# Order of the seven block products in the mLSTM query and key pairs

## The chip, the cores and the metric

The kernel runs on one core of a Trainium2 chip. The metric is device time of one execution, in microseconds (us). An engine works through its own list of instructions in the order in which the program put them; lists of different engines are tied together by semaphores. PE is the matrix engine, ACT the scalar engine, DVE the vector engine, SP the engine that issues the DMAs.

## The reference

The reference is one layer of a hybrid encoder block on 1024 tokens of width 1024, in float32. What matters here is its mLSTM branch: queries and keys are a projection of the normalised input, go through a causal convolution over four tokens and a SiLU, and then enter a chunkwise recurrence, four heads of width 128. Gates from the same projection scale the branches before they are merged.

```python
z = h @ w_in[i]
qa, ka, va, qk_m, vm, om, if_pre, ga, gb = jnp.split(z, split_pts, axis=-1)
...
qk_m = jax.nn.silu(causal_dwconv(qk_m, conv_m_w[i]))
qm, km = jnp.split(qk_m, 2, axis=-1)
...
hm = mlstm_chunkwise(qm.reshape(B, S, ML_HEADS, ML_DIM),
                     km.reshape(B, S, ML_HEADS, ML_DIM) * (ML_DIM ** -0.5),
                     vm.reshape(B, S, ML_HEADS, ML_DIM), i_pre, logf)
hm = head_layernorm(hm, ml_norm_g[i]) * jax.nn.sigmoid(om).reshape(B, S, ML_HEADS, ML_DIM)
```

## The kernel before, in words

Activations lie feature by token: 128 features on the partitions, 1024 tokens along the free axis, in two halves of 512. Two output tiles of 128 features are computed together, as a **pair**: for head h the query tile is row 0 of the pair, the key tile row 1. With the two halves of the tokens a pair has four outputs, (row, half). The pair is a 2x2 block product done with seven products (Strassen and Winograd's scheme) in place of eight. Each of the seven (`B11`, `T1`, `T2`, `B21`, `T3`, `B22`, `T4`) is a sum of 12 matmuls of 128x128 by 128x512: four blocks of the inner dimension, each three times (L379 weight high part by input high part, L380 weight high by input low, L381 weight low by input high), since every float32 operand is split into a high part (`wh`, by ACT, L121) and a remainder (`wl`, by DVE, L122).

`products` (L365) runs the seven on three PSUM banks. `B11`, then `T2`, `T3` and `T4` add into bank `b2`; `T1` and then `B22` into `b3`; `B21` into `b4`. The running sum in `b2` is read between them: after `B11` ACT copies it to the tile `s1`, after `T2` to `u2`, after `T3` DVE adds it to `s5` (the copy of `T1`), after `T4` it is an output. The outputs become complete with `B21` (row 0, half 0), `T3` (row 1, half 1), `B22` (row 0, half 1) and `T4` (row 1, half 0).

`left_operands` (L322) makes the weight side of each product in the order in which the products stand: it loads the four 128x512 weight blocks A11, A21, A22 and A12 of a pair into tiles `wr` (five buffers), forms the sums S1 to S4 on DVE (L292), and splits each operand into `wh` and `wl`, for which there are three buffers each. The eighth product of a stream of pairs thus reuses the buffer of the fifth.

`c_blocks` (L851) takes the four outputs. For a query and key pair (`make_qk`, L864) each output starts a convolution on DVE in `conv_silu` (L871, L874, and L877 for the tokens at the seam of the halves), a sigmoid on ACT (L880) and a product (L292 for queries, L884 for keys), into the tiles `cv`, one for the query and one for the key. The second half of a row needs the last three tokens of its first half. The key's second half lies in `s5` and waits until `T4` gives the first half, which ACT copies to the tile `c`. The tiles `s1`, `u2`, `s5` and `c` have one buffer each; the pair that comes next writes its own `s1` into the same place.

Each query and key pair is followed by a **gate pair** (two gate tiles, also by `c_blocks`), and that by the mLSTM head, whose scores `pS` (L941) multiply key by query. The first four scores need only the first halves of both. A scheduler sets the order of the instructions of each engine when the kernel is built; it moves instructions of independent work between each other, so that the scores stand inside the gate pair. There are four query and key pairs, at about 380, 451, 519 and 587 us.

Of the kernel before, what the change touches and what calls it, by code (L numbers as in the profile page):

```python
# [45 lines left out]
LO_M = "DDDDDDD"  # L46
# [8 lines left out]
T_Q, T_K, T_VA, T_QM, T_KM, T_VM, T_OM, T_GA, T_GB = 0, 4, 8, 12, 16, 20, 24, 28, 36  # L55
# [14 lines left out]
def block_kernel(ctx: ExitStack, tc: tile.TileContext, a: dict, out: bass.AP):  # L70
# [27 lines left out]
    def v(name, i=0, n=1):  # L98
        lo = _VEC_COLS[name][0] + i
        return vec[:, lo:lo + n]  # L100

    def acc(name):
        return pools["acc"].tile([P, HALF], F32, tag="acc", name=name)
# [9 lines left out]
    def half_slice(half):  # L113
        return slice(half * HALF, (half + 1) * HALF)
# [170 lines left out]
    BLOCKS_BY_USE = ("B11", "T1", "T2", "B21", "T3", "B22", "T4")  # L285
# [5 lines left out]
    def tt(eng, out, in0, in1, op):  # L291
        eng.tensor_tensor(out=out, in0=in0, in1=in1, op=op)  # L292

    def copy(out, ps):
        ACT.activation(out=out, in_=ps, func=AF.Copy)
# [8 lines left out]
    def new_blocks(n=KD // 2):  # L304
        return {m: [None] * n for m in BLOCKS}
# [16 lines left out]
    def left_operands(jobs):  # L322

        for src1, src2, n, engs, order in jobs:
            if src2 is None:
                for blk in order:
                    yield load_pre((src1, blk), n)
                continue

            def load(src):  # L330
                t = wr.tile([P, 4, P], F32, tag="wr", name="wr")[:, :n]
                SP.dma_start(out=t, in_=src)
                return t

            def comb(name, in0, in1, op=ALU.subtract):
                t = ws(n, name)
                tt(DVE, t, in0, in1, op)
                return t

            A11, A21, A22, A12 = load(src1[:, :n]), load(src2[:, :n]), load(src2[:, n:]), load(src1[:, n:])  # L340
            for blk in order:
                if blk == "T1":
                    S1 = comb("S1", A21, A22, ALU.add)
                    S2 = comb("S2", S1, A11)
                elif blk == "T3":
                    S3 = comb("S3", A11, A21)
                elif blk == "B22":
                    S4 = comb("S4", A12, S2)
                src = {"B11": lambda: A11, "T1": lambda: S1, "T2": lambda: S2, "B21": lambda: A12,
                       "T3": lambda: S3, "B22": lambda: S4, "T4": lambda: A22}[blk]()  # L350
                yield w_split(src, POOL if engs[BLOCKS_BY_USE.index(blk)] == "P" else DVE)
# [3 lines left out]
    def next_w():  # L355
        while len(w_queue) < 3:
            w_queue.append(next(left[0], None))
        return w_queue.pop(0)

    def start_products(jobs):  # L360

        left[:] = [left_operands(jobs)]
        w_queue[:] = [next(left[0]) for _ in range(2)]

    def products(blocks, order=BLOCKS_BY_USE):  # L365

        bank = {b: acc(b) for b in ("b2", "b3", "b4")}
        for blk in order:
            b = {"T1": "b3", "B22": "b3", "B21": "b4"}.get(blk, "b2")
            more = blk not in ("B11", "T1", "B21")
            w, rhs, n = next_w(), blocks[blk], len(blocks[blk])
            kw = dict(skip_group_check=True) if more else {}
            for k in range(n):
                (wh, wl), (xh, xl) = w[k], rhs[k]
                PE.matmul(bank[b], wh, xh, start=(k == 0 and not more), stop=False, **kw)  # L379
                PE.matmul(bank[b], wh, xl, start=False, stop=False, **kw)  # L380
                PE.matmul(bank[b], wl, xh, start=False, stop=(k == n - 1), **kw)  # L381
            yield blk, bank[b]
# [184 lines left out]
    with tc.tile_pool(name="att", bufs=1) as at:  # L567
# [210 lines left out]
        blocks = [(h, qb) for h in range(H) for qb in range(NTB)]  # L778
# [29 lines left out]
    zb = new_blocks()  # L808
# [18 lines left out]


    GATE_PAIRS = [(T_GA + 4, T_GA + 5), (T_GA + 6, T_GA + 7)] + [(T_GB + j, T_GB + j + 1) for j in range(0, KD, 2)]
    pair_jobs = [(T_QM, T_KM), GATE_PAIRS[0]]  # L830
    for h in range(H):
        pair_jobs.append((T_OM + h, T_GA + h))
        if h + 1 < H:
            pair_jobs.append((T_QM + h + 1, T_KM + h + 1))
        pair_jobs += GATE_PAIRS[h + 1:h + 2] if h + 1 < H else GATE_PAIRS[h + 1:]
    start_products([(a["w_in"][t1], a["w_in"][t2], 4, LO_M, BLOCKS_BY_USE) for t1, t2 in pair_jobs])

    hm_hl = [], []
    merged = new_blocks()
# [8 lines left out]
    def s_tile(tag, bufs=1):  # L848
        return mw.tile([P, HALF], F32, tag=tag, name=tag, bufs=bufs)

    def c_blocks(blocks, ready):  # L851

        s1, u2, s5 = s_tile("s1"), s_tile("u2"), s_tile("s5")
        for blk, ps in products(blocks):
            if blk in ("B11", "T1", "T2"):
                copy({"B11": s1, "T1": s5, "T2": u2}[blk], ps)
            elif blk == "T4":
                ready(1, 0, ps)
            else:
                t, row, half = {"B21": (s1, 0, 0), "T3": (s5, 1, 1), "B22": (u2, 0, 1)}[blk]  # L860
                tt(DVE, t, ps, t, ALU.add)
                ready(row, half, t)

    def make_qk(h):  # L864
        cvs = [mw.tile([P, S], F32, tag="cv", name="cv", bufs=3) for _ in range(2)]
        z = {}

        def conv_silu(row, half, prev):
            o, zt = cvs[row][:, half_slice(half)], z[row, half]
            i = h + 4 * row  # L870
            DVE.tensor_scalar(out=o, in0=zt, scalar1=v("cm", i * 4 + 3), scalar2=None, op0=ALU.mult)  # L871
            for j in (2, 1, 0):
                d, w = 3 - j, v("cm", i * 4 + j)
                DVE.scalar_tensor_tensor(out=o[:, d:], in0=zt[:, :HALF - d], scalar=w, in1=o[:, d:],  # L874
                                         op0=ALU.mult, op1=ALU.add)
                if half:
                    DVE.scalar_tensor_tensor(out=o[:, :d], in0=prev[:, HALF - d:], scalar=w, in1=o[:, :d],  # L877
                                             op0=ALU.mult, op1=ALU.add)
            sg = s_tile("sg", 2)
            ACT.activation(out=sg, in_=o, func=AF.Sigmoid)  # L880
            if row == 0:
                tt(DVE, o, o, sg, ALU.mult)
            else:
                DVE.scalar_tensor_tensor(out=o, in0=o, scalar=P ** -0.5, in1=sg, op0=ALU.mult, op1=ALU.mult)  # L884

        def ready(row, half, t):
            z[row, half] = t
            if row == 0:
                conv_silu(row, half, z[0, 0])
            elif half == 0:  # L890
                c21 = z[1, 0] = s_tile("c")
                copy(c21, t)
                conv_silu(1, 0, None)
                conv_silu(1, 1, c21)

        c_blocks(zb, ready)
        return cvs

    def gate_out(t, half, val):
# [7 lines left out]
    def gate_pair(t1, t2, om=None):  # L907

        def ready(row, half, t):
            if row == 0 and om is not None:  # L910
                ACT.activation(out=om[:, half_slice(half)], in_=t, func=AF.Sigmoid)
                return
            val = s_tile("c") if (row, half) == (1, 0) else t
            ACT.activation(out=val, in_=t, func=AF.Sigmoid)
            gate_out((t1, t2)[row], half, val)

        c_blocks(zb, ready)
# [71 lines left out]
    def mlstm_out(h, num):  # L989
# [11 lines left out]
        return om  # L1001

    qks = [make_qk(0)]
    gate_pair(*GATE_PAIRS[0])
    for h in range(H):
        num = mlstm_head(h)
        om = mlstm_out(h, num)
        if h + 1 < H:
            qks.append(make_qk(h + 1))
            gate_pair(*GATE_PAIRS[h + 1])  # L1010
    for h in range(H - 1):
# [6 lines left out]
    for c, parts in zip((H0, H1), hm_hl):  # L1018
        hi = mw.tile([P, HALF], F32R, tag="sg", name="hmh", bufs=2)
        split(hi, lo[:, c], om[:, c], lo_eng=DVE)  # L1020
        parts.append((hi, lo[:, c]))
    for pair in GATE_PAIRS[H:]:
        gate_pair(*pair)
# [409 lines left out]
```

## Time and profile before

| | us |
|---|---|
| three timed runs, median | 1595.6 |
| lowest and highest | 1594.05, 1598.84 |
| the profiled execution | 1594.36 |
| its span, first to last instruction | 1592.6 |
| PE busy in the span | 1544.1 |
| DVE busy | 1262.9 |
| ACT busy | 750.5 |

The profiled execution lies 1.2 us under the median and 1.8 us over its own span. Matmuls are pipelined: in a busy stretch they start closer together than one of them lasts, so time is read from starts.

### The profile page before, as it was taken

To read this page: it belongs to the slowest core of one execution; us is meant where nothing else is said; L and a number is where in the kernel's file an instruction comes from. 1 tells how busy PE (TensorE), PEld (TensorE's weight loads), DVE (VectorE), ACT (ScalarE), POOL (GpSimd) and SP (SyncE) were. 2 spreads that over 40 slices of the span, in tenths; PEclk is the share of its full clock that TensorE was granted. 3 is DMA by queue.
4 is the path that set the end of the run, shared out by engine and by line. 5 is a ranking of instruction groups with operands and counts; after the bars stand their busy time and mean duration, and the time that the engine had idled before them with its cause. 6 is when DMAs were issued, how large, how long until landed. Compare 5 with 4: busy or idle time off the path is not lost.

```text
span 1592.6 us, 21503 instructions
## 1 busy us (share of the span) xinstructions
PE 1544.1 (97%) x7413; PEld 1272.1 (80%) x7413; DVE 1262.9 (79%) x2193; ACT 750.5 (47%) x1448; POOL 26.0 (2%) x22
## 2 busy tenths in 40 slices
PE   8999999989999999999999999999999899999997
PEld 6777777867778788787877888888888778788997
DVE  6797885585888878759796888888888997878745
ACT  3465553444475564534365444444444635344522
POOL 0000000000000000000000000000000000000000
PEclk8999999989999999999999999999999999999999
DMA  5655641084424232465426333333333755332422
GB/s 188 193 172 172 199 143 41 21 281 150 132 74 140 95 116 86 139 225 181 149 88 223 106 106 106 105 101 99 100 100 106 244 160 185 106 131 60 136 88 90
DMA packets 117180, 212.58 MB, mean 133 GB/s; under 512 B 13840, under 2 KB 27728, under 8 KB 117072
## 3 DMA queue, kind: packets, MB, share of 16 engines
q1 hardware_dynamic: 116496, 210.70, 41.0%
q8 instruction: 58, 0.95, 0.3%
q10 hardware_dynamic: 576, 0.52, 0.1%
q14 instruction: 50, 0.41, 0.1%
HBM read 147.96 MB, written 59.02 MB: 130 GB/s over the span
## 4 chain that ended last, share of the span: by engine, by line
PE 71%; DVE 14%; DMA 6%; issue 4%; ACT 3%; SPq 1%; POOL 1%; DVEq 0%; POOLq 0%; ACTq 0%
PE b L381 18%; PE b L379 18%; PE b L380 17%; PE ps_pg L1333 2%; PE ps_pg L1335 2%; PE ps_pg L1334 2%; DVE wl L122 2%; DVE cv L874 1%; DVE mg L292 1%; PE pav L755 1%; PE ps_ya L150 1%; PE ps_ya L151 1%; PE ps_ya L152 1%; DVE nmax L728 1%; PE ps_s L706 1%
## 5 line engine op out<-in xcount | busy, mean ns | idle before, releaser
L379 PE MATMUL b<-T,wh 128*128 128x512 f32 x816 | 319.2, 391 | 6.6 <-ACT wh L121 2.8
L381 PE MATMUL b<-T,wl 128*128 128x512 f32 x816 | 318.9, 391 | 1.8 <-DVE wl L122 1.8
L380 PE MATMUL b<-T,wh 128*128 128x512 f32 x816 | 318.3, 390 | 0.0
L379 PE MATMUL b<-B,wh 128*128 128x512 f32 x612 | 239.9, 392 | 1.5 <-ACT wh L121 1.4
L381 PE MATMUL b<-B,wl 128*128 128x512 f32 x612 | 239.4, 391 | 1.2 <-DVE wl L122 0.7
L380 PE MATMUL b<-B,wh 128*128 128x512 f32 x612 | 238.5, 390 | 0.0
L121 ACT ACTIVATE wh<-S 128x512 fp32r<-128x512 f32 (+1 forms) x204 | 126.7, 621 | 233.9 <-PE b L380 209.8
L379 PEld LDWEIGHTS b<-T,wh 128*128 128x128 f32 x816 | 153.5, 188 | 41.4 <-ACT wh L121 4.6
L381 PEld LDWEIGHTS b<-T,wl 128*128 128x128 f32 x816 | 153.5, 188 | 35.6 <-DVE wl L122 3.6
L380 PEld LDWEIGHTS b<-T,wh 128*128 128x128 f32 x816 | 153.4, 188 | 32.1
L121 ACT ACTIVATE wh<-wr 128x512 fp32r<-128x512 f32 (+1 forms) x153 | 94.8, 621 | 163.5 <-PE b L380 105.9
L122 DVE TENSOR_TENSOR wl<-S,wh 128x512 fp32r<-128x512 f32 (+1 forms) x204 | 137.8, 676 | 39.3 <-ACT wh L121 38.1
L381 PEld LDWEIGHTS b<-B,wl 128*128 128x128 f32 x612 | 114.9, 188 | 26.5 <-DVE wl L122 1.9
L379 PEld LDWEIGHTS b<-B,wh 128*128 128x128 f32 x612 | 114.9, 188 | 26.4 <-ACT wh L121 2.2
L380 PEld LDWEIGHTS b<-B,wh 128*128 128x128 f32 x612 | 114.9, 188 | 23.7
L122 DVE TENSOR_TENSOR wl<-wr,wh 128x512 fp32r<-128x512 f32 (+1 forms) x153 | 103.3, 675 | 7.7 <-ACT wh L121 7.7
L292 DVE TENSOR_TENSOR x<-b,x 128x512 f32<-128x512 f32 x112 | 77.1, 689 | 34.5 <-PE b L381 34.1
L292 DVE TENSOR_TENSOR S<-wr 128x512 f32<-128x512 f32 (+1 forms) x102 | 69.1, 677 | 5.2 <-DMA wr<-w_o 3.3
L1169 DVE SCALAR_TENSOR_TENSOR ac<-ar,vec,ac 128x511 f32<-128x511 f32 (+1 forms) x88 | 65.8, 747 | 0.7
L709 ACT ACTIVATE e<-ps_s,nmax 128x128 f32<-128x128 f32 (+7 forms) x64 | 47.1, 738 | 35.3 <-DVE nmax L728 21.0
L1333 PE MATMUL ps_pg<-x,wpg 128*128 128x384 f32 (+1 forms) x192 | 61.3, 319 | 0.0
L1335 PE MATMUL ps_pg<-x,wpg 128*128 128x384 f32 (+1 forms) x192 | 61.0, 318 | 0.0
(309 smaller groups left out, 2810.4 us busy)
## 6 DMA issues: line engine op xcount, KB each, us to landing
wr<-w_up SPq DMA_DIRECT2D x84, 256.0 KB, 2.9
wr<-w_in SPq DMA_DIRECT2D x56, 256.0 KB, 3.0
pre<-pr SPq DMA_DIRECT2D x46, 256.0 KB, 2.3
wf<-w_in SPq DMA_DIRECT2D x32, 256.0 KB, 3.2
wr<-w_down SPq DMA_DIRECT2D x32, 256.0 KB, 2.8
wh<-pre SPq DMA_DIRECT2D x23, 256.0 KB, 4.2
wl<-pre SPq DMA_DIRECT2D x23, 256.0 KB, 4.5
xt<-xT SPq DMA_DIRECT2D x8, 512.0 KB, 6.6
```

The lines of the kernel that those rows point to most:

```text
L121: ACT.activation(out=hi, in_=src, func=AF.Copy)
L122: (lo_eng or DVE).tensor_tensor(out=lo, in0=src, in1=hi.bitcast(F32), op=ALU.subtract)
L150: PE.matmul(ps, wh, xh, start=(first and k == 0), stop=False)
L292: eng.tensor_tensor(out=out, in0=in0, in1=in1, op=op)
L379: PE.matmul(bank[b], wh, xh, start=(k == 0 and not more), stop=False, **kw)
L380: PE.matmul(bank[b], wh, xl, start=False, stop=False, **kw)
L381: PE.matmul(bank[b], wl, xh, start=False, stop=(k == n - 1), **kw)
L709: ACT.activation(out=e, in_=s_, func=AF.Exp, bias=nm[:, m:m + 1], scale=1.0, accum_out=rs[:, m:m + 1])
L1169: DVE.scalar_tensor_tensor(out=o[:, d:], in0=ar[:, j + d:j + HALF], scalar=v("cf", t * 3 + j), in1=o[:, d:], op0=ALU.mult, op1=ALU.add)
L1333: PE.matmul(pg, wh, xh[:, c], start=(i == 0), stop=False)
L1334: PE.matmul(pg, wh, xl[:, c], start=False, stop=False)
L1335: PE.matmul(pg, wl, xh[:, c], start=False, stop=(i == KD - 1))
```

## The change

The query and key pairs take their seven products in another order: `T3` and `T4`, which complete the key's two outputs, come before `B21` and `B22`, which complete the query's. All other pairs keep their order. The weight side is made in the new order too, since `left_operands` follows it.

```diff
@@ -827,13 +827,16 @@
+    QK_ORDER = ("B11", "T1", "T2", "T3", "T4", "B21", "B22")
     pair_jobs = [(T_QM, T_KM), GATE_PAIRS[0]]
...
-    start_products([(a["w_in"][t1], a["w_in"][t2], 4, LO_M, BLOCKS_BY_USE) for t1, t2 in pair_jobs])
+    start_products([(a["w_in"][t1], a["w_in"][t2], 4, LO_M, BLOCKS_BY_USE if t1 >= T_OM else QK_ORDER)
+                    for t1, t2 in pair_jobs])
...
-    def c_blocks(blocks, ready):
+    def c_blocks(blocks, ready, order=BLOCKS_BY_USE):
 
         s1, u2, s5 = s_tile("s1"), s_tile("u2"), s_tile("s5")
-        for blk, ps in products(blocks):
+        for blk, ps in products(blocks, order):
...
-        c_blocks(zb, ready)
+        c_blocks(zb, ready, QK_ORDER)
         return cvs
```

The number of instructions of each engine stays the same; their order changes in four places of the program, once for each query and key pair. In the rows below a name is a tile and its number, and `b2_4500<-T3_3648,wh_4522` reads: into bank `b2` of this pair, from the input block `T3` and the weight `wh`. The rows are from the second pair (head 1). Line numbers of the change are three higher than those of before from L831 on.

**First place: PE at the end of `T2`.** Before, the 12 matmuls of `B21` follow as a block:

```order
L381 MATMUL b2_4500<-T2_3592,wl_4504 128x512
L379 MATMUL b4_4502<-B21_3632,wh_4520 128x512
L380 MATMUL b4_4502<-B21_3632,wh_4520 128x512
L381 MATMUL b4_4502<-B21_3632,wl_4521 128x512
L379 MATMUL b4_4502<-B21_3636,wh_4520 128x512
```

Now two matmuls of `B21` (those that need only `wh`) stand first, then `T3`:

```order
L381 MATMUL b2_4500<-T2_3592,wl_4504 128x512
L379 MATMUL b4_4502<-B21_3632,wh_4556 128x512
L380 MATMUL b4_4502<-B21_3632,wh_4556 128x512
L379 MATMUL b2_4500<-T3_3648,wh_4522 128x512
L380 MATMUL b2_4500<-T3_3648,wh_4522 128x512
```

Behind these, PE now has the rest of `T3`'s 12, four of `B21`, all 12 of `T4`, the last six of `B21` and the 12 of `B22`. `B21`'s weight, the fourth operand of the pair before, is now the sixth.

**Second place: PE in the gate pair that follows,** where the first scores `pS` stand. Before, from the last matmul of `T1` on:

```order
L381 MATMUL b3_4677<-T1_3536,wl_4639 128x512
L379 MATMUL b2_4676<-T2_3577,wh_4679 128x512
L380 MATMUL b2_4676<-T2_3577,wh_4679 128x512
L379 MATMUL b4_4678<-B21_3632,wh_4696 128x512
L380 MATMUL b4_4678<-B21_3632,wh_4696 128x512
L941 MATMUL pS_4851<-cv_4495,cv_4496 128x128 x4
L381 MATMUL b2_4676<-T2_3577,wl_4680 128x512
L379 MATMUL b2_4676<-T2_3582,wh_4679 128x512
```

Now:

```order
L381 MATMUL b3_4677<-T1_3536,wl_4647 128x512
L379 MATMUL b4_4678<-B21_3632,wh_4696 128x512
L380 MATMUL b4_4678<-B21_3632,wh_4696 128x512
L944 MATMUL pS_4851<-cv_4495,cv_4496 128x128 x4
L379 MATMUL b2_4676<-T2_3577,wh_4679 128x512
L380 MATMUL b2_4676<-T2_3577,wh_4679 128x512
L381 MATMUL b2_4676<-T2_3577,wl_4680 128x512
L379 MATMUL b2_4676<-T2_3582,wh_4679 128x512
```

The two matmuls of `T2` that stood ahead of the scores have moved behind them.

**Third place: ACT and DVE ahead of that.** ACT before (`sg` is a sigmoid of the convolution `cv`, `s1_4673` the copy that `T2` of the gate pair waits for, query tile `cv_4495`, key tile `cv_4496`):

```order
L880 ACTIVATE sg_4631<-cv_4495 128x512
L295 ACTIVATE s1_4673<-b2_4676 128x512
L121 ACTIVATE wh_4715<-S3_4713 128x512
L880 ACTIVATE sg_4660<-cv_4496 128x512
L295 ACTIVATE s5_4675<-b3_4677 128x512
L880 ACTIVATE sg_4670<-cv_4496 128x512
```

ACT now:

```order
L121 ACTIVATE wh_4679<-S2_4644 128x512
L883 ACT_TABLE_LOAD
L883 ACTIVATE sg_4597<-cv_4496 128x512
L883 ACTIVATE sg_4607<-cv_4496 128x512
L121 ACTIVATE wh_4696<-wr_4616 128x512
L121 ACTIVATE wh_4715<-S3_4713 128x512
L295 ACTIVATE s5_4675<-b3_4677 128x512
L883 ACTIVATE sg_4639<-cv_4495 128x512
L883 ACTIVATE sg_4670<-cv_4495 128x512
L295 ACTIVATE s1_4673<-b2_4676 128x512
```

The copy into `s1` now stands behind both sigmoids of the query, and one table load with two sigmoids of the key stands ahead of them. On DVE, the last rows ahead of the split `wl_4680` were these of the key:

```order
L874 SCALAR_TENSOR_TENSOR cv_4496<-c_4654,vec_75,cv_4496 128x510
L874 SCALAR_TENSOR_TENSOR cv_4496<-s5_4499,vec_75,cv_4496 128x510
L874 SCALAR_TENSOR_TENSOR cv_4496<-c_4654,vec_75,cv_4496 128x509
L877 SCALAR_TENSOR_TENSOR cv_4496<-c_4654,vec_75,cv_4496 128x2
L874 SCALAR_TENSOR_TENSOR cv_4496<-s5_4499,vec_75,cv_4496 128x509
L884 SCALAR_TENSOR_TENSOR cv_4496<-cv_4496,sg_4660 128x512
L877 SCALAR_TENSOR_TENSOR cv_4496<-c_4654,vec_75,cv_4496 128x3
L122 TENSOR_TENSOR wl_4680<-S2_4636,wh_4679 128x512
```

They are now rows of the query, which read the old `s1` to the last:

```order
L877 SCALAR_TENSOR_TENSOR cv_4495<-s1_4497,vec_75,cv_4495 128x509
L880 SCALAR_TENSOR_TENSOR cv_4495<-s1_4497,vec_75,cv_4495 128x1
L877 SCALAR_TENSOR_TENSOR cv_4495<-u2_4498,vec_75,cv_4495 128x510
L292 TENSOR_TENSOR cv_4495<-cv_4495,sg_4639 128x512
L880 SCALAR_TENSOR_TENSOR cv_4495<-s1_4497,vec_75,cv_4495 128x2
L877 SCALAR_TENSOR_TENSOR cv_4495<-u2_4498,vec_75,cv_4495 128x509
L880 SCALAR_TENSOR_TENSOR cv_4495<-s1_4497,vec_75,cv_4495 128x3
L122 TENSOR_TENSOR wl_4680<-S2_4644,wh_4679 128x512
```

In the first pair, where the scores' eight exponentials (L934) and the sum of their mask (L932) fall into the same stretch, ACT had all eight behind the splits of the pair's seven weights; now five of them stand ahead of the split for `B22`. On SP the loads of `wb` and `xb` (L925, L930) for these now stand ahead of one weight load of the gate pair.

From the pair's first sum out of PSUM (`s1_4497<-b4_4502` before, `s5_4499<-b2_4500` now) to the row ahead of `wl_4680`, DVE had 31 instructions and now has 32: the sum S3 of the gate pair's weights, which stood just ahead of them, now stands among them.

## Rows read from the trace of the kernel before

**Rows 1.** page of the profile, busy time by engine: us, share, instructions

```profile
PE 1544.1 (97%) x7413; PEld 1272.1 (80%) x7413; DVE 1262.9 (79%) x2193; ACT 750.5 (47%) x1448; POOL 26.0 (2%) x22
```

**Rows 2.** waits of PE from 380 to 655 us: total us, times, longest

```profile
PE pS L941 <- DVE cv L884: 4.6, 3, 1.5
...
PE pS L941 <- issue: 2.7, 1, 2.7
```

**Rows 3.** timeline of PE, second pair and gate pair: start us, us

```profile
458.62 0.39 PE L380 MATMUL b<-T,wh 128*128 128x512 f32 x1
...
459.08 0.39 PE L379 MATMUL b<-B,wh 128*128 128x512 f32 x1
...
469.96 0.39 PE L379 MATMUL b<-B,wh 128*128 128x512 f32 x1
...
477.98 1.16 PE L941 MATMUL pS<-cv 128*128 128x128 f32 x8 [1.52 <-DVE cv L884]
...
478.90 0.48 PE L381 MATMUL b<-T,wl 128*128 128x512 f32 x1
479.21 0.39 PE L379 MATMUL b<-T,wh 128*128 128x512 f32 x1
```

**Rows 4.** timeline of ACT, first row first pair, others second

```profile
388.60 0.63 ACT L121 ACTIVATE wh<-S 128x512 fp32r<-128x512 f32 x1 [1.60 <-PE b L380]
...
459.05 0.64 ACT L121 ACTIVATE wh<-S 128x512 fp32r<-128x512 f32 x1 [1.24 <-PE b L380]
...
459.59 0.58 ACT L295 ACTIVATE u<-b 128x512 f32<-128x512 f32 x1
...
465.14 1.28 ACT L880 ACT_TABLE_LOAD   x1
...
466.55 0.63 ACT L880 ACTIVATE sg<-cv 128x512 f32<-128x512 f32 x1
...
473.19 0.62 ACT L880 ACTIVATE sg<-cv 128x512 f32<-128x512 f32 x1
...
473.71 0.58 ACT L295 ACTIVATE s<-b 128x512 f32<-128x512 f32 x1
```

**Rows 5.** timeline of DVE, second pair

```profile
462.00 0.69 DVE L292 TENSOR_TENSOR s<-b,s 128x512 f32<-128x512 f32 x1 [0.86 <-PE b L381]
...
472.68 0.49 DVE L871 TENSOR_SCALAR cv<-c,vec 128x512 f32<-128x512 f32 x1
473.07 0.22 DVE L877 SCALAR_TENSOR_TENSOR cv<-c,vec,cv 128x1 f32<-128x1 f32 x1
473.20 0.75 DVE L874 SCALAR_TENSOR_TENSOR cv<-c,vec,cv 128x511 f32<-128x511 f32 x1
473.87 0.69 DVE L292 TENSOR_TENSOR cv<-cv,sg 128x512 f32<-128x512 f32 x1
474.47 0.75 DVE L874 SCALAR_TENSOR_TENSOR cv<-c,vec,cv 128x510 f32<-128x510 f32 x1
...
477.98 0.69 DVE L122 TENSOR_TENSOR wl<-S,wh 128x512 fp32r<-128x512 f32 x1
```

**Rows 6.** timeline of DVE, ACT and PE, one row each, first pair

```profile
392.42 1.22 DVE L932 TENSOR_TENSOR xb<-xb,mask 128x1024 f32<-128x1024 f32 x1
...
393.68 2.46 ACT L934 ACTIVATE xb<-xb,mg 128x128 f32<-128x128 f32 x8 [1.72 <-DVE xb L932]
...
410.77 0.39 PE L379 MATMUL b<-T,wh 128*128 128x512 f32 x1
```

**Rows 7.** timeline of PE, ahead of the four pairs

```profile
331.91 0.47 PE L150 MATMUL ps_ya<-hi,wh 128*128 128x512 f32 x1 [2.44 <-issue]
```

**Rows 8.** stretches: length, busy (count) of five engines, granted clock, DMA share, GB/s

```profile
340.00:343.00 3.00, 3.00 (x7) 2.42 (x8) 3.00 (x6) 1.80 (x3) 0.00 (x0) 0.50 0.76 258
...
380.47:409.58 29.11, 25.82 (x114) 20.79 (x112) 22.03 (x41) 15.32 (x29) 0.00 (x0) 1.00 0.25 84
```

**Rows 9.** page of the profile, DMA issues: count, KB each, us to landing

```profile
wr<-w_in SPq DMA_DIRECT2D x56, 256.0 KB, 3.0
```


## Prediction

> **What bounds the kernel now.** I began with the busy times: PE works 1544.1 of 1592.6 us [rows 1], so a change that adds no work can only give back or add PE's waits. The list of PE's waits over the stretch of the four pairs is short: three waits of the scores for the key's product on DVE, 4.6 us together, and one of 2.7 us in the first pair put down to "issue" [rows 2]. The timelines show what lies behind them. In the second pair PE stands still until the scores start at 477.98, since DVE has worked without a gap from 462.00, when the pair's first sum became ready, to the split at 477.98 [rows 3, 5]. So in this stretch DVE's queue sets the end, not PE, and the question is when that queue starts and what stands last in it.
>
> **The scale.** From 459.08 to 469.96 PE starts 48 matmuls [rows 3]: 0.227 us each. From engine to engine it takes 0.04 us: the matmul that starts at 458.62 ends at 459.01, and ACT starts at 459.05 [rows 3, 4]. After a wait PE's second start comes 0.31 us after the first (478.90, 479.21), 0.08 more than in the flow. I write the second pair out in time; the third and fourth repeat it.
>
> **First step, the weight of `B21`: a new wait.** Three weight buffers serve seven operands. As the sixth, `B21` takes the buffer of `T2`, whose last reader ends at 459.01; ACT's split takes 0.64 us, to 459.69 [rows 3, 4]. Two matmuls of `B21` stand next in PE's queue, so they start at 459.73, not 459.08, and everything behind them waits along. `T3` then starts at 460.27. It also needs the copy to `u2`, which ends at 460.17 (459.59 + 0.58) [rows 4] and so costs nothing more; it was covered by all of `B21` before, and is now covered by the split. Without the wait `T3` could have started at 459.53: 0.74 us lost. `T3` is through at 462.99, its last matmul ends at 463.15, and DVE's sum runs from 463.19 to 463.88 (0.69, as at 462.00 [rows 5]). `T4` needs it; the four matmuls of `B21` between them last to 463.90 and cover it, with nothing to spare. Thirty matmuls later, at about 470.74, the gate pair starts, 0.8 us later than at 469.96 [rows 3]. That is this step's price, in each of four pairs.
>
> **Second step, DVE's queue: starts later and grows.** It starts at 463.19, not 462.00: the first sum now needs `T3`, not `B21`. A plain tensor operation takes 0.60 us from start to start (473.87 to 474.47), a long convolution step 0.67 (473.20 to 473.87), the scaling 0.39, the seam 0.13 [rows 5]. The 31 instructions of before (9, 12, 4 and 6 of these) make 15.8 of the measured 15.98 us; the rest is dependence. Now there are 32, the S3 sum among them: 16.58. The nineteen ahead of the key's first product take 9.98 (7 at 0.60, 6 at 0.67, 3 each at 0.39 and 0.13, and 0.2), to 473.17. Its sigmoid has to come by then. On ACT it stands behind a weight split, which waits for `B22`'s last reader (470.68) and ends at 471.36, and behind the table load; from that load's start to the sigmoid's it is 1.41 us, and the sigmoid takes 0.63 [rows 4]. So it ends at 473.40 and DVE waits 0.27. The queue reaches its last row at 479.91 and the split behind it at 480.04, against 477.98.
>
> [...] The row of before shows the sigmoid 0.13 us after the load's end, so I go by the row.
>
> **Third step, what releases PE.** The scores need both first halves. The key's is ready; the query's product is the fourth row from the end of DVE's queue, starts at 478.51 and ends at 479.20. PE comes there at 476.63 (26 matmuls after 470.74) and waits 2.6 us, where it waited 1.5. The scores last 0.92 us (477.98 to 478.90 [rows 3]), to 480.16. Next is `T2` of the gate pair, which needs the copy of `b2` to `s1`. There is one `s1`, and the query's second half reads the old one in DVE's last row, which ends at 480.13. Behind that ACT has a sigmoid, and the copy starts 0.52 us after it (473.19, 473.71) and takes 0.58 [rows 4]: 481.27. PE waits again, 1.15 us. Three matmuls of `T2` are through at 482.08; before, at 479.21 [rows 3]. The second pair loses 2.87 us, three pairs 8.6.
>
> **The first pair** lies 70.45 us earlier (388.60 for 459.05 [rows 4]). Its eight exponentials took 2.46 us from 393.68, behind the mask's sum at 392.42 [rows 6]; five of them, 1.54 us, now stand ahead of the split for `B22`, whose remainder is the second row of DVE's queue. The exponentials can start between 392.5 and 393.68, so that remainder comes at 394.7 to 395.9, not at 393.34: 1.3 to 2.5 us late, less the 0.27 us that DVE then no longer waits. `T2`'s three are through at 412.7 to 413.9, against 410.77 [rows 6]: 1.9 to 3.1 us. The xb load is issued earlier than before, so I take 2.4, a little under the middle.
>
> **What costs nothing.** Weight loads land 3.0 us after issue [rows 9]. The one that moves behind `wb` and `xb` on SP feeds `B21` of the gate pair, whose remainder DVE makes only behind its whole queue; without that cover it would cost those 3 us. The loads of `ya` wait on SP for the sigmoid tiles and move with the query's products; only DVE's gate products wait for them, off PE's path.
>
> **The sum.** 8.6 + 2.4 = 11.0 us on an execution of 1594.36: 1605.4. The median of the timed runs lies 1.2 above that execution, so I forecast **1606.6 us**; its own range is 1603 to 1610.
>
> **Rivals.**
> [...]
> [...]
> Smaller loss: DVE's queue runs closer than my pitches or ACT's sigmoids come sooner, and only the first step stays: 4 x 0.8 = 3.2, 1598.8 us.
> Not slower: the scores no longer wait. `T4` does end 18 matmuls earlier (66 instead of 84 into the pair). Then 7.3 us come back [rows 2] and 3.2 go: 1591.5. It decides at 476.63: the query's product would have to end there, 2.6 us before I have it, and `s1` be free 3.5 us earlier. DVE has no gap of that size from 463.19 on, which speaks against it.
>
> **Numbers.** Forecast 0.61, clock 0.20, smaller loss 0.12, not slower 0.07. A measurement of this kernel can tell about 0.3%, 4.8 us, from no change: the bounds are 1590.8 and 1600.4. The smaller loss lies mostly inside it (0.09), the last rival half (0.03): same 0.12, faster 0.04, slower 0.84. The range of 1599 to 1615 leaves out the last rival, part of the smaller loss and a fall in more than two pairs.
>
> **What would show it.** In the profile after: PE waits of about 0.65 us for a `wh` split between `T2` and `B21`, in four places; scores that wait about 2.6 us for a product of L292, not of the key's line; `T2` waiting about 1.2 us for the copy to `s1`, four times; DVE busy without a gap from the sum after `T3` to the gate pair's split; a clock of 1.00 throughout. I am wrong if the scores start without a wait, if `T2` doesn't wait for `s1`, or if the clock row falls.

## The result and the profile after

The changed kernel took 1614.96 us (median of four runs, 1613.82 to 1616.86) beside 1595.74 for the kernel before: a ratio of 1.0117, interval 1.0100 to 1.0134. It is 19.2 us slower, where the sum gave 11.0. The profiled execution has a span of 1612.0 us.

The page of the changed kernel, busy time by engine and the granted clock in 40 slices (beside [rows 1]):

```profile
PE 1555.3 (96%) x7413; PEld 1277.5 (79%) x7413; DVE 1263.3 (78%) x2193; ACT 748.3 (46%) x1448; POOL 26.0 (2%) x22
...
PEclk8999999999999999999999999999999999999998
```

PE does the same 7413 matmuls and is "busy" for 11.2 us more. That busy time can grow without more work is the first sign that matmuls ran slower somewhere. The slices, 40 us each, are too wide to show it.

The waits of PE in the changed kernel over the four pairs (beside [rows 2]):

```profile
PE pS L944 <- DVE cv L292: 7.1, 3, 2.4
PE b L379 <- ACT s L295: 3.5, 4, 1.0
PE pS L944 <- issue: 2.4, 1, 2.4
PE b L379 <- ACT wh L121: 2.0, 4, 0.5
```

The scores wait for the query's product (L292), three times 2.4 us and in the first pair as "issue"; `T2` of the gate pair waits for the copy to `s1` and `B21` for its `wh`, four times each. The timeline of PE in the second pair (beside [rows 3]):

```profile
461.00 0.39 PE L380 MATMUL b<-T,wh 128*128 128x512 f32 x1
...
462.11 0.50 PE L379 MATMUL b<-B,wh 128*128 128x512 f32 x1 [0.49 <-ACT wh L121]
...
479.00 0.39 PE L380 MATMUL b<-B,wh 128*128 128x512 f32 x1
481.75 1.16 PE L944 MATMUL pS<-cv 128*128 128x128 f32 x8 [2.37 <-DVE cv L292]
483.88 0.80 PE L379 MATMUL b<-T,wh 128*128 128x512 f32 x1 [0.97 <-ACT s L295]
484.48 0.63 PE L380 MATMUL b<-T,wh 128*128 128x512 f32 x1
484.90 0.63 PE L381 MATMUL b<-T,wl 128*128 128x512 f32 x1
```

The row at 461.00 answers to that at 458.62 before, so this pair lies 2.38 us later. `B21` starts at 462.11, 0.65 us later than that alone would make it. The scores start at 481.75, `T2` at 483.88. Behind it the matmuls start 0.43 us apart, not 0.23, though nothing waits. ACT and DVE in the same pair (beside [rows 4, 5]):

```profile
461.43 0.63 ACT L121 ACTIVATE wh<-wr 128x512 fp32r<-128x512 f32 x1 [1.43 <-PE b L380]
...
473.95 1.28 ACT L883 ACT_TABLE_LOAD   x1
475.25 1.15 ACT L883 ACTIVATE sg<-cv 128x512 f32<-128x512 f32 x2
...
482.71 0.63 ACT L883 ACTIVATE sg<-cv 128x512 f32<-128x512 f32 x1 [1.74 <-DVE cv L880]
483.25 0.58 ACT L295 ACTIVATE s<-b 128x512 f32<-128x512 f32 x1
```

```profile
465.65 0.69 DVE L292 TENSOR_TENSOR s<-b,s 128x512 f32<-128x512 f32 x1 [2.87 <-PE b L381]
...
475.91 0.69 DVE L887 SCALAR_TENSOR_TENSOR cv<-cv,sg 128x512 f32<-128x512 f32 x1 [0.17 <-ACT sg L883]
...
481.00 0.69 DVE L292 TENSOR_TENSOR cv<-cv,sg 128x512 f32<-128x512 f32 x1
...
482.41 0.21 DVE L880 SCALAR_TENSOR_TENSOR cv<-s,vec,cv 128x3 f32<-128x3 f32 x1
482.54 0.68 DVE L122 TENSOR_TENSOR wl<-S,wh 128x512 fp32r<-128x512 f32 x1
```

The first sum on DVE starts at 465.65, 1.27 us late against the shift; the split behind the queue's end at 482.54, 2.18 late (before: 477.98). The query's product starts at 481.00 and releases the scores; the last row that reads the old `s1` starts at 482.41, and ACT's copy, behind one more sigmoid, at 483.25.

Stretches of 8 us from the start of the scores (length; busy time and count of PE, weight loads, DVE, ACT, POOL; granted clock; DMA share; GB/s), first in the first and second pair of the kernel before:

```profile
409.58:417.58 8.00, 8.00 (x39) 6.79 (x40) 8.00 (x14) 3.02 (x5) 0.00 (x0) 1.00 0.30 98
477.98:485.98 8.00, 8.00 (x39) 6.80 (x40) 8.00 (x14) 3.06 (x6) 0.00 (x0) 1.00 0.33 100
```

In the four pairs of the changed kernel, and 2 us within the second:

```profile
407.53:415.53 8.00, 7.14 (x22) 5.60 (x23) 5.72 (x11) 1.93 (x4) 0.00 (x0) 0.57 0.32 98
481.75:489.75 8.00, 7.03 (x28) 5.74 (x29) 6.60 (x12) 2.23 (x4) 0.00 (x0) 0.79 0.32 100
484.50:486.50 2.00, 2.00 (x6) 1.62 (x5) 2.00 (x4) 0.00 (x0) 0.00 (x0) 0.50 0.38 123
554.48:562.48 8.00, 7.32 (x23) 5.77 (x24) 5.72 (x11) 1.89 (x4) 0.00 (x0) 0.57 0.34 99
627.85:635.85 8.00, 7.03 (x27) 5.64 (x28) 6.40 (x12) 2.23 (x4) 0.00 (x0) 0.79 0.32 100
```

The granted clock is 0.50 from 484.5 to 486.5, and all four pairs have such a stretch (0.50 also from 411 to 413, 557 to 559 and 631 to 633). Before, the third and fourth stretch stand at 1.00 too. PE had been still for 2.4 us ahead of the scores, and was again for 0.7 to 1.0 us behind them.

In two pairs the fall did not need both waits. PE in the first and the third pair:

```profile
407.53 1.23 PE L944 MATMUL pS<-cv 128*128 128x128 f32 x8 [2.42 <-issue]
409.62 0.80 PE L379 MATMUL b<-T,wh 128*128 128x512 f32 x1 [0.86 <-ACT s L295]
...
554.48 1.45 PE L944 MATMUL pS<-cv 128*128 128x128 f32 x8 [2.37 <-DVE cv L292]
556.61 0.79 PE L379 MATMUL b<-T,wh 128*128 128x512 f32 x1 [0.68 <-ACT s L295]
```

The scores last longer than the 1.16 us of the second pair, and the granted clock is 0.50 from 408.45 to 409.62 and from 555.30 to 555.90: here it was down before the second wait began. In the second and fourth pair it fell during the second wait and just behind it (0.82 from 482.91 to 483.88; 1.00 from 629.01 to 629.98, then 0.80 to 630.50 and 0.50).

**Where the time is.** One stretch holds all four pairs: from the last matmul of the first pair's `T2` to the last `pn` of the fourth head. Its ends in the kernel before, and in the changed one (the second row of each is a group: first and last start):

```profile
388.40 0.39 PE L381 MATMUL b<-T,wl 128*128 128x512 f32 x1
...
L954 PE MATMUL pn<-C,wb x14: 273/275/316, 632.6 to 636.6; 128*128 128x129 f32 x14
```

```profile
386.96 0.39 PE L381 MATMUL b<-T,wl 128*128 128x512 f32 x1
...
L957 PE MATMUL pn<-C,wb x14: 272/275/314, 649.1 to 653.1; 128*128 128x129 f32 x14
```

636.6 - 388.40 = 248.2 us before, 653.1 - 386.96 = 266.1 now: 17.9 of the 19.4 us between the two spans lie here. I call it the stage. The changed kernel comes to it 1.4 us earlier and takes 2.9 us more behind it; why is not shown. The stage is the better measure below, since the time outside it differs as well: taken as the difference of the medians less that of the stage, by 2.1 us less to 3.3 us more than before.

### The profile page after: what moved, and what is told of

It reads as the page before. It is cut to its first block, busy times and chain, and to the rows that moved or that the text cites. A ratio compares the mean times of both kernels' runs of the same rounds, so it can differ in the third digit from the quotient of the medians.

```text
span 1612.0 us, 21505 instructions
## 1 busy us (share of the span) xinstructions
PE 1555.3 (96%) x7413; PEld 1277.5 (79%) x7413; DVE 1263.3 (78%) x2193; ACT 748.3 (46%) x1448; POOL 26.0 (2%) x22
## 4 chain that ended last, share of the span: by engine, by line
PE 75%; DVE 10%; DMA 7%; issue 3%; ACT 3%; SPq 1%; POOL 0%; DVEq 0%; POOLq 0%; ACTq 0%
PE b L379 19%; PE b L381 19%; PE b L380 18%; PE ps_pg L1336 2%; PE ps_pg L1338 1%; PE ps_pg L1337 1%; DVE mg L292 1%; PE pav L755 1%; PE ps_s L706 1%; PE ps_ya L150 1%; DVE cv L877 1%; PE ps_ya L151 1%; DVE wl L122 1%; PE ps_ya L152 1%; ACT e L709 1%
## 5 line engine op out<-in xcount | busy, mean ns | idle before, releaser
L379 PE MATMUL b<-T,wh 128*128 128x512 f32 x816 | 323.3, 396 | 10.7 <-ACT s L295 4.3
L381 PE MATMUL b<-T,wl 128*128 128x512 f32 x816 | 322.3, 395 | 1.8 <-DVE wl L122 1.8
L380 PE MATMUL b<-T,wh 128*128 128x512 f32 x816 | 321.7, 394 | 0.0
L379 PEld LDWEIGHTS b<-T,wh 128*128 128x128 f32 x816 | 155.3, 190 | 48.9 <-ACT s L295 5.7
L380 PEld LDWEIGHTS b<-T,wh 128*128 128x128 f32 x816 | 155.5, 191 | 32.4
L292 DVE TENSOR_TENSOR x<-b,x 128x512 f32<-128x512 f32 x112 | 77.0, 688 | 35.0 <-PE b L381 34.9
L292 DVE TENSOR_TENSOR S<-wr 128x512 f32<-128x512 f32 (+1 forms) x102 | 68.9, 676 | 5.8 <-DMA wr<-w_o 4.5
```

## The experiments

Each was timed beside the kernel before. "Against before" is the difference of the medians, "stage" the difference of the stage to 248.2 us in one profiled execution, and "matmuls" the counts of PE in the four stretches of 8 us from the start of the scores (from the `T2` or `B21` that waits, where the scores wait for 0.2 us or not at all). The profiled execution lies 3.3 us under the median in e5 and 5.9 us in e9, so there the stage may say too little.

| kernel | median | against before | ratio, interval | stage | matmuls |
|---|---|---|---|---|---|
| the change | 1615.0 | +19.2 | 1.0100 to 1.0134 | +17.9 | 22, 28, 23, 27 |
| e1 two `s1` | 1607.3 | +11.2 | 1.0047 to 1.0088 | +9.4 | 30, 29, 29, 36 |
| e2 four `wh` | 1611.5 | +15.4 | 1.0074 to 1.0121 | +17.5 | 28, 23, 27, 22 |
| e3 scores late | 1615.6 | +19.5 | 1.0097 to 1.0144 | +17.0 | 28, 29, 25, 29 |
| e4 filled wait | 1607.6 | +11.4 | 1.0052 to 1.0091 | +9.7 | 34, 34, 34, 34 |
| e5 `T4` alone | 1606.8 | +9.1 | 1.0036 to 1.0076 | +7.2 | 35, 28, 35, 28 |
| e6 scaling on ACT | 1605.9 | +8.3 | 1.0033 to 1.0073 | +10.3 | 28, 28, 28, 28 |
| e7 before, scaling on ACT | 1592.9 | -4.8 | 0.9959 to 0.9985 | -6.3 | |
| e8 `T4` alone, scaling on ACT | 1596.0 | -1.7 | 0.9978 to 1.0002 | -0.6 | 35, 35, 35, 35 |
| e9 before, filled | 1604.6 | +7.7 | 1.0028 to 1.0065 | +4.4 | |
| e10 half filled | 1610.2 | +13.3 | 1.0072 to 1.0113 | +11.5 | 34, 34, 34, 28 |
| e11 two `s1`, filled | 1600.7 | +3.8 | 1.0008 to 1.0036 | +5.3 | 35, 35, 35, 35 |
| e12 two `s1`, scaling on ACT | 1595.2 | -1.7 | 0.9979 to 1.0005 | -1.4 | 35, 35, 35, 35 |

**The clock: e4, e10, e9.** Work that counts for nothing is put into the wait of the scores:

```diff
+            if half == 0:
+                for _ in range(2):
+                    PE.matmul(pS, kT[:, :P], kT[:, hs], start=True, stop=True)
```

> The changed kernel with two useless float32 matmuls of key by key, 128x512, into the bank of the scores ahead of the first four scores of each head (the scores then overwrite them, so nothing of the result changes). Four scores of 128x128 take 0.92 us, so these two should take about 1.84 us, and they stand in the wait of 2.4 us. Theory A (the clock falls because PE stands still there): the scores start when they did, their wait shrinks to about 0.6 us, the clock stays at 1.00, and more work makes the kernel faster by up to 7.7 us: 1607 to 1610. Rival F (the low clock has another reason than PE's idle time): the same low stretches, and 1615 or a little more.

PE in the second pair of e4, and the four stretches:

```profile
477.74 1.88 PE L944 MATMUL pS<-cv 128*128 128x512 f32 x4
480.26 1.16 PE L947 MATMUL pS<-cv 128*128 128x128 f32 x8 [0.65 <-DVE cv L292]
482.39 0.50 PE L379 MATMUL b<-T,wh 128*128 128x512 f32 x1 [0.97 <-ACT s L295]
```

```profile
408.52:416.52 8.00, 7.02 (x34) 5.82 (x35) 7.98 (x14) 2.87 (x5) 0.00 (x0) 1.00 0.30 98
480.26:488.26 8.00, 7.03 (x34) 5.82 (x35) 7.98 (x14) 2.87 (x5) 0.00 (x0) 1.00 0.34 100
551.42:559.42 8.00, 7.02 (x34) 5.83 (x35) 7.99 (x14) 2.87 (x5) 0.00 (x0) 1.00 0.32 99
622.29:630.29 8.00, 7.03 (x34) 5.84 (x35) 8.00 (x14) 2.87 (x5) 0.00 (x0) 1.00 0.28 98
```

The two fillers run for 1.88 us from 477.74, the scores still wait 0.65 for the query's product, `T2` still 0.97 for `s1`, and the clock is 1.00 in all four stretches. They hold 136 matmuls where the changed kernel has 100; 36 x 0.227 = 8.2 us. By the stage the fillers win 8.2 us as well, by the medians 7.8. More work made the kernel faster: PE stood still for 0.65 us ahead of the scores, not 2.37, and kept its clock. This shows the clock's part; what stays, 9.7 us in the stage, I put down to the waits.

> The changed kernel with one useless matmul of 0.92 us in place of two ahead of the scores, so that PE stands still about 1.5 us there and 1 us behind the scores. Theory A: no work that counts moves, so only the clock can tell: if PE's idle time decides it, the clock falls in fewer pairs or for a shorter time than in the changed kernel, and the time lies between 1607.5 and 1615, about 1611. Rival (any wait of the scores near a wait for s1 is enough): low in all four pairs, 1615.

With one filler the waits are 1.51 and 0.97 us in each pair. The last of the four stretches in e10:

```profile
623.15:631.15 8.00, 7.02 (x28) 5.69 (x29) 6.66 (x12) 2.24 (x4) 0.00 (x0) 0.79 0.31 98
```

Three pairs keep the clock, the fourth loses 6 matmuls; 1610.2 us, as theory A had it.

> A control for the filled wait: the kernel before with the same two useless matmuls (1.84 us together) ahead of the first four scores of each head. Its waits there are 1.5 us in three pairs and 2.7 us in the first, and the clock was 1.00 there, so there is nothing to win. Theory A: the fillers end 0.3 us behind the wait in three pairs, so about 1 us is lost, within 2 us of the kernel before. Rival F (the fillers win by something else than the clock, such as a shift of what comes behind): several us faster than the kernel before, as they were on the changed kernel.

This control missed. PE in the second pair of e9:

```profile
479.27 1.13 PE L941 MATMUL pS<-cv 128*128 128x512 f32 x2 [1.51 <-DVE cv L884]
```

The fillers need the key's product, which is the very thing that the kernel before waits for [rows 2]. They stand behind the wait of 1.51 us, not in it, and the scores move out of their place. The stage grew by 4.4 us, with the clock at 1.00 in all four pairs, and the median by 7.7; where the rest of the median's loss lies is not shown. So it shows that the fillers win nothing by themselves, but is no clean control: what they cost was mis-sized.

**The copy to `s1`: e1, e11.**

```diff
-        return mw.tile([P, HALF], F32, tag=tag, name=tag, bufs=bufs)
+        return mw.tile([P, HALF], F32, tag=tag, name=tag, bufs=2 if tag == "s1" else bufs)
```

> The changed kernel with two buffers for the tile s1 and nothing else. Theory A (the three waits, and a clock that falls because the wait of the scores and the wait for the copy to s1 lie close together): T2 of the gate pair no longer waits about 1 us for the copy, and two of its matmuls (0.45 us) move into the wait of the scores, so 1.4 us a pair or 5.7 us come back; the scores still wait about 2 us and the granted clock stays at 1.00, which gives back another 7.7 us: about 1601.5. Rival B (the long wait of the scores alone brings the clock down): only the 5.7 us, about 1609, with low stretches behind the scores as before. Rival C (s1 only looks like the reason, the remainder from the end of DVE's queue comes no earlier): T2's third matmul waits as long as T2 did, and the time stays within 2 us of 1615.

PE in the second pair of e1:

```profile
477.84 1.16 PE L944 MATMUL pS<-cv 128*128 128x128 f32 x8 [1.91 <-DVE cv L292]
479.36 0.50 PE L381 MATMUL b<-T,wl 128*128 128x512 f32 x1 [0.37 <-DVE wl L122]
```

Two matmuls of `T2` again stand ahead of the scores, and the third waits only 0.37 us, for its remainder. Rival B comes nearest, with 1609: the wait went, as both had it, but the clock still fell in three of the four pairs (0.79 in their stretches, 1.00 in the fourth's), behind 1.9 us at the scores and 0.4 us at `T2` (20 matmuls short of four times the fourth's 36, 4.5 us). Without the clock 4.9 of the 9.7 us are left.

> The changed kernel with two buffers for s1 and the two useless matmuls. With two buffers alone it took 1607.3 us, with low clock in three of four pairs for 3 us each. Theory A: the fillers take the 1.9 us in which the scores wait, the clock stays at 1.00 in the four pairs, and what is left of the loss is the weight's wait and the late queue: 1615 less 5.7 less about 8, 1601 to 1603. Rival (the two remedies take the same time out): no more than either alone, 1607.

With the fillers too the clock is 1.00 and the stage stands at +5.3, which agrees with those 4.9. So of the stage's 17.9 us the single `s1` costs about 4.6 and the clock 8.2, and some 5 are left for `B21`'s weight and the late queue, which no run tells apart. The median, 1600.7, is a little under what theory A gave.

**The wait of the scores: e3.** The transposes of the key go ahead of the scores:

```diff
-            pS, pk = acc("pS"), acc("pk")
+            pk, pS = acc("pk"), acc("pS")
...
-                PE.matmul(pS[:, cs], kT[:, cg], qT[:, cg], start=True, stop=True)
                 PE.transpose(pk[:, cs], kT[:, cg], ident)
...
+                PE.matmul(pS[:, cs], kT[:, cg], qT[:, cg], start=True, stop=True)
```

> The changed kernel with the transposes of the key ahead of the scores in the program, by which the scores move behind the gate pair and nothing there waits for the query's product. Theory A: the waits stand in a row, so without the first the second grows: T2 of the gate pair then waits some 3.5 us for the copy to s1 instead of 1, and starts no earlier than now; PE's idle time is the same or longer, the clock still falls, and the time stays within 3 us of 1615. Rival E (the wait of the scores for the query's product is itself the loss): 4 x 2.4 = 9.6 us come back, about 1605.

```profile
479.90 0.60 PE L944 MATMUL pk<-ident,cv 128*128 128x128 f32 x4
484.55 0.80 PE L379 MATMUL b<-T,wh 128*128 128x512 f32 x1 [4.06 <-ACT s L295]
```

In the second pair of e3, above, no score waits, and `T2` waits 4.06 us for the copy to `s1` in its place. The median did not change (1615.6 for 1615.0): the waits stand in a row, and the loss is no property of the scores.

**The weight of `B21`: e2.** A fourth buffer, from a pool of its own, for every fourth split:

```diff
+        n_split[0] += 1
+        pool = wq[0] if n_split[0] % 4 == 0 else wp
-        wh = wp.tile([P, 4, P], F32R, tag="wh", name="wh")[:, :n]
+        wh = pool.tile([P, 4, P], F32R, tag="wh", name="wh")[:, :n]
```

> The changed kernel with a fourth buffer for the weight's high part and remainder, used by every fourth split, so that B21 as the sixth product reuses the buffer of a product that is long done. Theory A: the four waits of B21 for its weight (0.5 to 0.65 us) are gone, T3 and with it DVE's queue start about 0.7 us earlier, the scores with them: 4 x 0.7 = 3 us come back, and the two waits near the scores and the low clock stay, about 1612. Rival D (this wait is what brings the whole delay, since everything behind it moves with it): the waits of the scores and for s1 shrink to what they were before, and over 8 us come back, under 1607.

The wait for `wh` is gone, but the stage is nearly as long as in the changed kernel (+17.5): neither theory's gain. With the weight there, the scheduler put five matmuls of `B21` and `B22` ahead of `T3`, not two. DVE's first sum in the second pair of e2:

```profile
467.35 0.69 DVE L292 TENSOR_TENSOR s<-b,s 128x512 f32<-128x512 f32 x1 [3.49 <-PE b L383]
```

`T2`'s last matmul starts at 462.67 there, so this is 4.68 us behind it; in the changed kernel it is 465.65 - 461.23 = 4.42. The queue started no earlier, and the price of the weight's wait alone stays open. Against the kernel before e2 stands 3.8 us better than the change by the medians; nearly all of that lies outside the stage.

**The order in part: e5.**

```diff
-    QK_ORDER = ("B11", "T1", "T2", "T3", "T4", "B21", "B22")
+    QK_ORDER = ("B11", "T1", "T2", "B21", "T3", "T4", "B22")
```

> Part of the change alone: the order B11, T1, T2, B21, T3, T4, B22, in which only T4 moves ahead of B22 and B21 keeps its place. Theory A (DVE's queue sets when PE goes on; it starts at its old time if B21 is fourth, B21's weight finds a free buffer, and s1 still comes free with the queue's last row): no wait for B21's weight, no wait of the scores (the key's product comes earlier, the query's first as in the kernel before), but T2 of the gate pair waits some 1.5 us for the copy to s1, so 0.5 us a pair is lost against the kernel before and the clock stays at 1.00: about 1598. Rival H (that the query's second half now ends the queue is the trouble, wherever B21 stands): the scores still wait over 2 us, the clock falls, and the time is near 1610.

PE in the second pair of e5, and the row of DVE that it waits for:

```profile
475.87 1.05 PE L944 MATMUL pS<-cv 128*128 128x128 f32 x8
479.24 0.50 PE L381 MATMUL b<-B,wl 128*128 128x512 f32 x1 [2.32 <-DVE wl L122]
```

```profile
478.49 0.69 DVE L122 TENSOR_TENSOR wl<-wr,wh 128x512 fp32r<-128x512 f32 x1
```

The scores indeed run without a wait, but both theories missed the place of the next: a third matmul of `B21` now stands ahead of `T2`, and its remainder `wl` is split on DVE only behind the whole queue. PE stands still for 2.3 us in each pair, in two of them the clock falls (0.79 in the stretch; 14 matmuls, 3.2 us), and the stage loses 7.2 us, not 2. That DVE's queue sets the time is borne out; what of PE waits for its end depends on the order that the scheduler makes.

**The length of DVE's queue: e6, e7, e8, e12.** The four scalings of a pair go to ACT:

```diff
-            DVE.tensor_scalar(out=o, in0=zt, scalar1=v("cm", i * 4 + 3), scalar2=None, op0=ALU.mult)
+            ACT.activation(out=o, in_=zt, func=AF.Copy, scale=v("cm", i * 4 + 3))
```

> The kernel before with the four scalings of each pair's convolutions made by ACT instead of DVE, and nothing else. Theory A: the waits of the scores in the second to fourth pair (1.5 us each) go, that of the first pair (2.7 us) shrinks by 1.6, so 6 us come back: about 1590. Rival G: DVE then waits for ACT, whose copies and sigmoids stand in the same list, and the time stays within 2 us of that of the kernel before.

PE's waits for the scores in e7:

```profile
PE pS L941 <- issue: 1.1, 1, 1.1
PE pS L941 <- DVE cv L884: 0.8, 3, 0.3
```

The three waits of 1.5 us have shrunk to 0.3 or less, the first from 2.7 to 1.1. The stage is 6.3 us shorter, the median 4.8: a ratio of 0.9972, below 1 over its whole interval. This one beats both kernels, with the old order.

> The changed kernel with the four scalings of each pair's convolutions (0.39 us each on DVE) made by ACT instead, so DVE's queue is 1.6 us shorter. Theory A (the length of that queue sets both waits): the scores wait 0.8 us instead of 2.4, three matmuls of B21 stand between the scores and T2, whose wait for s1 falls to about 0.3 us; 2.3 us a pair come back, 9 in all, and the clock stays up, which gives back 7 to 8 more: about 1598. Rival G (the waits hang on ACT's sigmoids and on when PE's sums come, not on the length of DVE's queue): within 3 us of 1615.

On the changed kernel the gain came only in part. The second pair of e6:

```profile
475.76 1.16 PE L944 MATMUL pS<-cv 128*128 128x128 f32 x8
478.74 0.70 PE L381 MATMUL b<-B,wl 128*128 128x512 f32 x1 [1.82 <-DVE wl L122]
```

The scores follow at once, but `B21` waits for its `wl` as in e5, 1.82 us, and against theory A the clock fell in all four pairs (0.79 in each stretch), behind this one wait: 28 matmuls fewer than 4 x 35, 6.4 us. Without the clock the stage would stand at +3.9.

> The order with T4 alone ahead of B22 (B21 fourth) together with the scalings on ACT. Theory A: DVE's queue starts at its old time and is 1.6 us shorter, so the copy to s1 comes when PE is there, and neither the scores nor T2 wait for more than some tenths of a us: all 7.3 us of waits of the kernel before come back, about 1589, the clock at 1.00. Rival H (the query's second half at the end of the queue keeps s1 too long): T2 still waits over 1 us, about 1595.

Here the same wait is 1.57 us in the second pair, the clock stays at 1.00 in all four, and the kernel is no slower than before, nor faster. Theory A's 1589 was missed for the reason seen in e5. Rival H's 1595 fits the time, but what waits is `B21` for its remainder, not `T2` for `s1`.

> The changed kernel with two buffers for s1 and the four scalings of each pair on ACT. Theory A: both waits near the scores shrink to some tenths of a us, the clock stays at 1.00, only the wait of B21 for its weight stays: 1615 less 5.7, less 4 x 1.6, less about 8, some 1595, still 2 to 3 us behind the kernel before with its scalings on ACT (1592.9). Rival (the new order carries a further cost in the stage): over 1600.

The time is as theory A had it, 1595.2 us, with the clock at 1.00; the wait for the remainder is 1.0 us in the second pair, where some tenths were expected. Against e7, the same edit on the old order, the new order still loses 4.9 us in the stage.

## Why the prediction was right, and where its size was wrong

Slower was right, and the steps stood as written but for the sizes below. What failed is the clock: the forecast had it at 1.00, and named a fall in the clock row as a sign that it is wrong; the row fell. The sum's 1606.6 us is 8.4 us short. That 1614.96 still lies inside the stated range, by 0.04 us, is luck: the range left out a fall in more than two pairs, and the clock fell in four, at 2.1 us each.

- **First step.** `B21` starts 0.65 us late, as worked out, with the same wait in all four pairs. In the second the gate pair starts at 473.33, 0.99 us late against 469.96 [rows 3], where 0.8 was worked out. What this wait costs at the end could not be had by itself, since e2 changed the order with it.
- **Second step.** DVE's first sum was to come 1.19 us late and came 1.27; DVE's wait for the key's sigmoid was to be 0.27 and is 0.17 (475.91); the split behind the queue was to be 2.06 late and is 2.18. On the table load: ACT's sigmoid starts 1.30 us behind the load's start (473.95, 475.25), 1.41 before.
- **Third step.** The scores were to start at 479.24 in the time of before and did at 481.75 - 2.38 = 479.37; `T2` at 481.31 and did at 481.50. The 2.6 us forecast for the scores' wait counts from PE's next start, the 1.5 beside it from the end of the last matmul; counted like the 1.5 it is 2.45, and 2.37 was measured. With its first starts at the pace of [rows 3] the fourth matmul of `T2` would have started at 484.65, 3.06 us late; the sum had 2.87.
- **First pair.** Its 2.4 us were too much. DVE's row for the mask came 2.55 us earlier than before (at 388.43, in the time of before 389.87, for 392.42 [rows 6]), so the five exponentials were through when the split for `B22` was due and held up nothing. `T2` starts at 409.62 in a pair that lies 1.44 us earlier (386.96 for 388.40); its three are through 0.77 us later at full pace, 411.83 in the time of before against 410.77 [rows 6]: 1.1 us.
- **The sum.** 3 x 3.06 + 1.1 = 10.3 us, predicted 11.0; with the clock held up by the fillers the stage measured 9.7 and the medians 11.4.
- **The clock.** The forecast had 1.00 throughout; a fall in one or two pairs had a chance of 0.20. It fell in all four. I read the first pair's 2.7 us without a fall [rows 8] as a sign against it, though in the kernel before the granted clock had gone from 1.00 ahead of 331.90 to 0.50 from 334 to 343, behind the 2.44 us at 331.91 [rows 7]. The first pair's row of [rows 8] ends where the wait ends and can't show what follows; the stretch behind it, from 409.58, does stand at 1.00. I looked for a fall where two waits come close together; in the first and third pair the wait of the scores was enough (0.50 from 408.45 and from 555.30). The range's upper end, 1615, has room for two falls of 4 us, an estimate of mine from 8 us at the half pace of [rows 8]; no run shows that price. By the counts of matmuls each of the four falls in the changed kernel cost 8.2 / 4 = 2.1 us on average. That PE's standing still brings the fall on is shown by the fillers: with them the clock was 1.00 in all four pairs of e4 and e11 and in three of e10, where without them it was 0.57 to 0.79 in the changed kernel and 0.79 in three pairs of e1. Why the same wait brings it on at one time and not at another stays open, see below.

The two waits in the gate pair are one delay: the queue of DVE ends later, and what waits for its rows comes one after another. Taking away the wait of the scores moved it (e3, and in part e5 and e6); shortening the queue (e6, e7, e12), or freeing what its last row holds (e1), took time out. `B21`'s wait for its weight comes ahead of the queue, and taking it away left the stage as it was (e2).

## What to carry to other kernels

Before an order of products is changed, ask which engine's queue sets the next start, and write out the queue's last rows: the buffers they read, and the splits behind them. An order that finishes one output earlier won nothing here, since another output's rows then ended that queue; moving work off the queue did (e7). Where PE will stand still for some 2 us, price the clock with the wait: by the counts of matmuls a fall cost 1.4 us (e10) to 2.1 us (the change) on average.

## What was not expected of the hardware

The granted clock did not follow the length of a wait alone. A wait of 2.69 us left it at 1.00 in the kernel before, while 1.82 us in e6 were followed by a fall in all four pairs, 2.3 us in e5 in two of four, 1.9 with 0.4 us in e1 in three of four, 1.5 with 1.0 us in e10 in one of four, and 1.57 us in e8 in none (0.79 in each stretch where it fell, 1.00 where not). With 2.4 and 0.7 to 1.0 us in the changed kernel (0.57 to 0.79), or 4.1 in one piece in e3 (0.69 to 0.82), it fell every time. Each of these is one profiled execution; the waits of e3, e6 and e8 are those of the second pair. So by the counts of matmuls waits like these cost 1.4 to 2.1 us more than themselves in some pairs and nothing more in others; with what chance, one execution's profile doesn't tell. And 1.88 us of useless matmuls for each head were worth 8.2 us in the stage.
